# Four edits to a fused decoder layer: modulation sums split evenly between two engines, an early activation table, a divided half load, and two row blocks through other buffers

## The chip, the cores and the metric

The kernel runs on one core of one Trainium2 chip. The metric is the device time of one execution in microseconds (us), the median of several runs. Work is given to five engines that run side by side and wait for each other through semaphores: PE (matmuls), DVE and POOL (elementwise), ACT (activations and copies), and SP, which here issues the DMA transfers.

## The reference

One layer of a hybrid decoder on x (2048 x 1024, fp32) with a conditioning vector c:

```python
mod = jax.nn.silu(c) @ w_ada[layer] + b_ada[layer]
sh1, sc1, g1, sh2, sc2, g2 = jnp.split(mod[:, None, :], 6, axis=-1)
h = x * (1.0 + sc1) + sh1
proj = h @ w_in[layer] + b_in[layer]
...   # sliding-window attention and spatial gating on proj, joined to mixed
y = mixed @ w_out[layer]
x = layer_norm(ALPHA * x + g1 * y, ln1_g[layer], ln1_b[layer])
h = x * (1.0 + sc2) + sh2
gate, up = jnp.split(h @ w_gate_up[layer], 2, axis=-1)
y = (jax.nn.silu(gate) * up) @ w_down[layer]
x = layer_norm(ALPHA * x + g2 * y, ln2_g[layer], ln2_b[layer])
```

## The kernel before

All large products are done in three passes: each fp32 operand is split into a high part (a rounding copy, ACT, `split_hi`, L138) and a low part (the difference, DVE, `split_lo`, L141), and `mm3` (L144 to L146) issues high x high, one mixed product and the other mixed product, 128 x 128 by 128 x 512, into one PSUM bank.

The stages in order of time: a startup that makes the first two modulation vectors (`sh1`, `sc1`) in eight pieces k = 0 to 7 (`ada_ss`) and multiplies the first 512 rows of h with six column groups of the input weights, one k after the other (18 matmuls of 512 columns per k, 144 in all); a loop over the other rows with attention and gating; the out projection with the first LayerNorm, tile by tile (t = 0 to 15); the FFN's first product in two halves of the rows, each 11 steps `it` of seven products i = 0 to 6 (a Strassen-like scheme, products numbered n = 7 it + i); and the down product, a loop over seven combinations p with eight row blocks m each, 33 matmuls a block.

`ada_ss(k)` multiplies eight 128 x 256 weight pieces with c. For k = 0 all eight pieces are summed on PE, in 16 matmuls with one column; for the others DVE sums the first six (L225, L227), and PE does the last two and DVE's sum (L231, L233), six matmuls for two columns of output. L234 adds the bias; then `make_h` scales x (L193 on DVE) and splits it. Before the first product PE runs warm-up matmuls, 12 and then 8 (L323, L328), and a small product for the bias table (L325, copied by ACT at L326 and stored to `br_d`).

In the FFN `h_tiles(last_h2)` turns the last tiles of h over to the layout of the products: transposes on PE (L858) and eight copies on ACT (L861). It stands behind the product n = 0. `prep(n)` makes the weight combination of product n and its split two products ahead, `load_h(hf, i)` loads and splits the operand of product i in two pieces through a ring of two buffers (`hraw`: one in XF, and G1B). Between the halves `load_h(1, i)` follows each product of step it = 10. L1016 copies the accumulator Xg out of PSUM after a product; the first Silu is at L999.

In the down product `aprep(p, m)` loads row block m of operand p from `ac_d` through a ring of two buffers in F and splits it, one block ahead; `y_load` loads the residual rows into the tiles y. The FFN's last stores to `ac_d` and the weights' loads (L1106) are on the same queue.

The order of work on each engine is made by a scheduler from the program order, the buffers and its own priorities, except where `tc.keep_in_program_order` pins an instruction. Each engine executes its list in order; SP issues its transfers in order too, and a transfer is issued only when the eighth before it has landed.

Of the kernel before, what the change touches and what calls it, by code (L numbers as in the profile page):

```python
# [9 lines left out]
F32 = mybir.dt.float32  # L10
F32R = mybir.dt.float32r
U32 = mybir.dt.uint32
AF = mybir.ActivationFunctionType
ALU = mybir.AluOpType
# [10 lines left out]
WB = 255  # L25
# [32 lines left out]
def tile_layer(ctx, tc, xT, x, cT, wada_ss, wada4, bada_p, bada_g, win_g, win_a,  # L58
# [47 lines left out]
    def small(n, tag):  # L106
        return smalls.tile([P, n], F32, tag=tag, name=tag)
# [15 lines left out]
    expo = const(8)  # L123
# [11 lines left out]
    og = CS2[:, 22:30]  # L135

    def split_hi(hi, src, eng=None, **kw):
        (eng or A).activation(hi, src, AF.Copy, **kw)  # L138

    def split_lo(lo, src, hi, eng=None):  # L140
        (eng or V).tensor_tensor(lo, src, hi.bitcast(F32), op=ALU.subtract)  # L141

    def mm3(ps, lh, ll, rh, rl, start, stop, **kw):
        T.matmul(ps, lh, rh, start=start, stop=False, **kw)  # L144
# [60 lines left out]
    def load_wg(j, dst, pr, eng, r):  # L205
        r = load(r, win_g[j * 4 + pr])
        for i in range(2):
            hi, lo = dst[2 * pr + i]
            src = r[:, i * 512:(i + 1) * 512]
            split_hi(hi, src)  # L210
            split_lo(lo, src, hi, eng)

    def ada_ss(k):

        nd = 6 if k else 0
        ps = PS[7][:, 0:2]
        if k == 0:
            SY.dma_start(bap, bada_p)
            V.tensor_scalar(bap[:, 0:8], bap[:, 0:8], 1.0, None, op0=ALU.add)
            V.tensor_scalar(bap[:, 16:24], bap[:, 16:24], 1.0, None, op0=ALU.add)  # L220
        r = [load(ra0(), wada_ss[k, hf]) for hf in range(2)]
        piece = [r[rc // 4][:, rc % 4 * 256:rc % 4 * 256 + 256] for rc in range(8)]
        if nd:
            av = accs()
            V.tensor_scalar(av, piece[0], c_s[:, 0:1], None, op0=ALU.mult)  # L225
            for rc in range(1, nd):
                V.scalar_tensor_tensor(av, piece[rc], c_s[:, rc:rc + 1], av, op0=ALU.mult, op1=ALU.add)  # L227
        for j in range(2):
            js = slice(j * 128, (j + 1) * 128)
            for rc in range(nd, 8):  # L230
                T.matmul(ps[:, j:j + 1], piece[rc][:, js], c_s[:, rc:rc + 1], start=rc == nd, stop=rc == 7 and not nd)  # L231
            if nd:
                T.matmul(ps[:, j:j + 1], av[:, js], ones[:, 0:1], start=False, stop=True)  # L233
        V.tensor_tensor(mod.rearrange("p (j k) -> p k j", j=4)[:, k, 0:2], ps,  # L234
                        bap.rearrange("p (j k) -> p k j", j=4)[:, k, 0:2], op=ALU.add)

# [29 lines left out]
    def proj(ps, hT, t, k, w):  # L266
        hi, lo, _ = hT[k]
        mm3(ps, hi[:, t * 128:(t + 1) * 128], lo[:, t * 128:(t + 1) * 128], w[k][0], w[k][1],
            k == 0, k == KC - 1)
# [48 lines left out]
    SY.dma_start(relx, rel)  # L318
    SY.dma_start(ohx[:, 0:WB], onehot)
    warm = hbuf[7][2]  # L320
    V.memset(warm[:, 0:640].bitcast(F32), 0.0)
    for _ in range(12):
        T.matmul(PS[6], warm[:, 0:128], warm[:, 128:640], start=True, stop=True)  # L323
    prep0(0)
    T.matmul(PS[7][0:8, 256:256 + WB], relx, ohx[:, 0:WB], start=True, stop=True)  # L325
    A.activation(bstage, PS[7][0:8, 256:256 + WB], AF.Copy, scale=8.0)  # L326
    for _ in range(8):
        T.matmul(PS[6], wgv[0][0][:, 0:128], wgv[0][0], start=True, stop=True)  # L328
    for k in range(KC):
        if k + 1 < KC:  # L330
            prep0(k + 1)
        for t in range(6):
            proj(tiles0[t], hT, t % 4, k, wgv if t < 4 else wgu_)
    tc.keep_in_program_order(SY.dma_start(br_d, bstage))
    start_pool.__exit__(None, None, None)
    late_pool = tc.tile_pool(name="late", bufs=1)
# [493 lines left out]
    def load_h(hf, i, ring=hraw):  # L830
        hi, lo = HO[i]
        for h in range(2):
# [3 lines left out]
            split_hi(hi[:, hs], r)  # L836
            split_lo(lo[:, hs], r, hi[:, hs])

    def ln_stats(r):
        st, mv, rs = small(12, "st"), small(2, "mv"), small(1, "rstd")  # L840
        for h in range(2):
            V.bn_stats(st[:, h * 6:(h + 1) * 6], r[:, h * 512:(h + 1) * 512])
        V.bn_aggr(mv, st)
        V.tensor_scalar(rs, mv[:, 1:2], EPS, None, op0=ALU.add)  # L844
        G.tensor_tensor(rs, rs, expo[:, 0:1], op=ALU.pow)  # L845
        return mv, rs
# [64 lines left out]
    for t in range(NPRE, NT):  # L911
        if t + 1 < NT:
            stage_a(t + 1)
        r, xr, mx = loads[t]
        res = rr()
        st8 = wo_steps(t, xr, mx, res)
        for s_ in st8[0:8]:
            s_()
        if t + 1 < NT:
            mix_tr(loads[t + 1][0], loads[t + 1][2])  # L920
        for s_ in st8[8:16]:
            s_()
        h_tiles(ready)
        ready = []
        ln1(t, res)
        ready.append((t, res))
        if early:
            e = early.pop(0)
            re = rr()
            SY.dma_start(re, x1_d[e * P:(e + 1) * P, :])  # L930
            ln1(e, re)
            ready.append((e, re))
        if 3 < t < 12:
            rc = t - 4
            r = XF[:, 0:1024]
            SY.dma_start(r, wada4[3, rc])
            if rc == 0:
                V.tensor_scalar(G2B, r, c_s[:, 0:1], None, op0=ALU.mult)
            else:
                V.scalar_tensor_tensor(G2B, r, c_s[:, rc:rc + 1], G2B, op0=ALU.mult, op1=ALU.add)  # L940
            if rc == 7:
                SY.dma_start(r, bada_g[1:2, :].to_broadcast([P, D]))
                for h in range(2):
                    ps = trr()
                    T.matmul(ps, ones, G2B[:, h * 512:(h + 1) * 512], start=True, stop=True)
                    V.tensor_tensor(G2B[:, h * 512:(h + 1) * 512], ps, r[:, h * 512:(h + 1) * 512], op=ALU.add)
        if t in (10, 12):
            load_h(0, (t - 10) // 2, Ring([XF[:, 1024:2048]]))
    last_h2 = ready
# [102 lines left out]
    for n in range(NIT * 7):  # L1052
        it, i = divmod(n, 7)
        if n + 2 < NIT * 7:
            prep(n + 2)
        hi, lo = asl[n % 3]
        hh, hl = HO[i]
        for g in range(2):
            for j in range(4):
                ws = slice(g * 512 + j * 128, g * 512 + (j + 1) * 128)  # L1060
                hs = slice(j * 512, (j + 1) * 512)
                mm3(banks4[i][g], hi[:, ws], lo[:, ws], hh[:, hs], hl[:, hs],
                    first[i] and j == 0, j == 3, skip_group_check=not first[i])
        if n == 0:
            trr = Ring(PS[6:8])
            h_tiles(last_h2)
        post(n)
        if it == 10:
            load_h(1, i)
        fold_wd(i, it)  # L1070


# [45 lines left out]
        split_hi(hi, r)  # L1118
        split_lo(lo, r, hi)

    def aprep(p, m):
        r = arw()
        SY.dma_start(r, ac_d[p, m])
        hi, lo = at_()
        split_hi(hi, r)
        split_lo(lo, r, hi)
        return hi, lo

    def final(half, m, tail):
# [21 lines left out]
        tg = tile_of(half, m)  # L1151
        tc.keep_in_program_order(SY.dma_start(y[half][m], x1_d[tg * P:(tg + 1) * P, :]))

    nxt = aprep(seq[0], 0)
    for c in range(11):
        bsplit(0, c, bsum(0, c))
    y_load(1, 0)
# [2 lines left out]
    for n, p in enumerate(seq):  # L1160
        sums = []
        for m in range(8):
            ah, al = nxt
            if m < 7:
                nxt = aprep(p, m + 1)
            elif n < 6:
                nxt = aprep(seq[n + 1], 0)
            if n == 0:
# [98 lines left out]
```

## Time and profile before

| what | value |
|---|---|
| runs shown | 1971.59, 1974.17, 1976.45 us; median 1974.17 |
| profiled execution | 1973.5 us |
| its span, first to last instruction | 1971.5 us |
| PE busy | 1938.2 us (98%) |
| DVE, ACT busy | 1332.1 us (68%), 786.7 us (40%) |
| mean granted clock of PE | 0.99 |
| DMA | 354 MB on SP's queue, mean 180 GB/s |

The profile shows one execution. Rows of a timeline have the start and the duration in us, the engine, the source line, the operation, output and inputs, the shape and the count, and in brackets the idle time ahead with what ended it. SPq are SP's issues of transfers. Matmuls overlap, so their durations are longer than the distance of their starts. A one-column matmul of fp32 makes two records.

### The profile page before, as it was taken

The page shows a single profiled execution, that of the slowest core. Times are in us where ns is not written, and L with a number is a line of the kernel's source. Part 1 is how long each engine was busy: PE and PEld are TensorE (multiplying, and loading weights), DVE is VectorE, ACT ScalarE, POOL GpSimd, SP SyncE. Part 2 cuts the span into 40 slices and gives each one's busy share as a digit, 9 for nine tenths or more (in the row PEclk, how much of TensorE's full clock was granted, in tenths as well). Part 3 has the DMA queues.
Part 4 walks back from the last instruction along what each step waited for, and adds up shares of the span by engine and source line. Part 5 has one row for each costly group of instructions (what it writes and reads, how often), then busy time and mean ns, then how long its engine had stood idle before and what let it go on. Part 6 is the DMA issues. An engine that isn't in the chain of part 4 may idle for free.

```text
span 1971.5 us, 23966 instructions
## 1 busy us (share of the span) xinstructions
PE 1938.2 (98%) x8740; PEld 1585.2 (80%) x8740; DVE 1332.1 (68%) x2077; ACT 786.7 (40%) x1365; POOL 321.9 (16%) x285
## 2 busy tenths in 40 slices
PE   9999999999999999999999999999999899999998
PEld 7878878888878788888888788888888688888886
DVE  6675677996598776656666766566556665558856
ACT  3463346674355543333334433333334232224422
POOL 0545513564343100000000000000000000002303
PEclk8999999999999999999999999999999999999999
DMA  8763563533499764443445644434445985555623
GB/s 336 275 222 142 177 228 114 202 97 113 167 318 311 224 218 134 133 129 123 134 123 182 208 134 124 139 114 136 134 124 175 341 290 198 175 174 195 225 94 124
DMA packets 218399, 355.09 MB, mean 180 GB/s; under 512 B 14593, under 2 KB 124329, under 8 KB 218281
## 3 DMA queue, kind: packets, MB, share of 16 engines
q1 hardware_dynamic: 218280, 353.56, 54.0%
q8 instruction: 68, 1.11, 0.2%
q14 instruction: 51, 0.41, 0.1%
HBM read 242.88 MB, written 111.68 MB: 180 GB/s over the span
## 4 chain that ended last, share of the span: by engine, by line
PE 85%; DVE 6%; DMA 5%; ACT 2%; issue 2%; POOL 0%; SPq 0%; DVEq 0%; ACTq 0%; POOLq 0%
PE PS L144 26%; PE PS L146 26%; PE PS L145 26%; PE PS L626 2%; DVE R L141 2%; DMA RAW<-in_wada_dram 1%; ACT R L138 1%; PE PS L607 1%; PE PS L560 1%; PE PS L561 1%; DMA F<-ac_d 1%; DMA XF<-in_wada_dram 1%; DMA RAW<-in_xT_dram 1%; PE PS L858 1%; DMA G1B<-ht_d 0%
## 5 line engine op out<-in xcount | busy, mean ns | idle before, releaser
L145 PE MATMUL PS<-R 128*128 128x512 f32 (+1 forms) x1416 | 553.2, 391 | 0.3 <-DVE R L141 0.3
L144 PE MATMUL PS<-R 128*128 128x512 f32 (+1 forms) x1240 | 485.3, 392 | 9.3 <-ACT R L138 5.0
L146 PE MATMUL PS<-R 128*128 128x512 f32 (+1 forms) x1240 | 479.3, 389 | 3.3 <-DVE R L141 3.3
L145 PEld LDWEIGHTS PS<-R 128*128 128x128 f32 x1416 | 268.6, 190 | 56.7 <-DVE R L141 0.5
L141 DVE TENSOR_TENSOR R<-RAW,R 128x1024 fp32r<-128x1024 f32 (+1 forms) x212 | 217.6, 1041 | 126.6 <-ACT R L138 123.8
L138 ACT ACTIVATE R<-RAW 128x1024 fp32r<-128x1024 f32 (+1 forms) x232 | 202.8, 885 | 244.1 <-PE PS L145 191.6
L144 PEld LDWEIGHTS PS<-R 128*128 128x128 f32 x1240 | 235.5, 190 | 62.2 <-ACT R L138 7.3
L144 PE MATMUL PS<-R,R 128*128 128x512 f32 x688 | 275.1, 400 | 2.5 <-ACT R L138 1.3
L146 PEld LDWEIGHTS PS<-R 128*128 128x128 f32 x1240 | 233.8, 189 | 53.2 <-DVE R L141 5.0
L145 PE MATMUL PS<-R,R 128*128 128x512 f32 x688 | 273.6, 398 | 0.0
L146 PE MATMUL PS<-R,R 128*128 128x512 f32 x688 | 270.3, 398 | 0.3 <-DVE R L141 0.3
L845 POOL TENSOR_TENSOR rstd<-rstd,CS 128x1 f32<-128x1 f32 x32 | 35.3, 1105 | 1257.2 <-DVE rstd L844 1257.2
L144 PE MATMUL PS<-HA,R 128*128 128x512 f32 x528 | 208.7, 396 | 2.9 <-ACT R L138 2.9
L146 PE MATMUL PS<-HA,R 128*128 128x512 f32 x528 | 207.9, 395 | 0.4 <-DVE R L141 0.4
L138 ACT ACTIVATE R<-F 128x1408 fp32r<-128x1408 f32 (+2 forms) x86 | 105.4, 1229 | 226.5 <-PE PS L145 221.1
L144 PEld LDWEIGHTS PS<-R,R 128*128 128x128 f32 x688 | 130.4, 190 | 32.3 <-DMA R<-h_d 1.7
L146 PEld LDWEIGHTS PS<-R,R 128*128 128x128 f32 x688 | 130.0, 189 | 30.1 <-DVE R L141 0.7
L145 PEld LDWEIGHTS PS<-R,R 128*128 128x128 f32 x688 | 130.5, 190 | 28.4 <-issue 0.2
L141 DVE TENSOR_TENSOR R<-F,R 128x1408 fp32r<-128x1408 f32 (+2 forms) x86 | 132.0, 1537 | 22.9 <-ACT R L138 22.9
L145 PE MATMUL PS<-HA,R 128*128 128x512 f32 x352 | 138.9, 395 | 0.0
L1186 DVE TENSOR_TENSOR y<-y,PS 128x512 f32<-128x512 f32 x96 | 62.1, 682 | 104.5 <-PE PS L146 104.4
L969 DVE TENSOR_TENSOR F<-F,PS 128x512 f32<-128x512 f32 x132 | 89.8, 681 | 53.9 <-PE PS L146 52.6
(237 smaller groups left out, 2605.1 us busy)
## 6 DMA issues: line engine op xcount, KB each, us to landing
RAW<-in_wgu_dram SPq DMA_DIRECT2D x88, 512.0 KB, 3.9
ac_d<-fc SPq DMA_DIRECT2D x154, 256.0 KB, 2.6
F<-ac_d SPq DMA_DIRECT2D x56, 704.0 KB, 4.2
RAW<-wdg_d SPq DMA_DIRECT2D x100, 256.0 KB, 5.4
h_d<-R SPq DMA_DIRECT2D x32, 512.0 KB, 4.3
R<-h_d SPq DMA_DIRECT2D x32, 512.0 KB, 6.6
RAW<-in_wada_dram SPq DMA_DIRECT2D x24, 512.0 KB, 3.6
XF<-in_wd_dram SPq DMA_DIRECT2D x22, 512.0 KB, 4.5
```

Source lines behind the costliest of these rows:

```text
L138: (eng or A).activation(hi, src, AF.Copy, **kw)
L141: (eng or V).tensor_tensor(lo, src, hi.bitcast(F32), op=ALU.subtract)
L144: T.matmul(ps, lh, rh, start=start, stop=False, **kw)
L145: T.matmul(ps, lh, rl, start=False, stop=False, **kw)
L146: T.matmul(ps, ll, rh, start=False, stop=stop, **kw)
L560: T.matmul(b3[:, j, o:256], qh[:, qc], khh[kv][:, kc], start=True, stop=False)
L561: T.matmul(b3[:, j, o:256], qh[:, qc], klo[kv][:, kc], start=False, stop=True)
L607: T.transpose(tp[:, g * 128:(g + 1) * 128], p3[:, g, :], ident)
L626: T.matmul(psav, lh, rh, start=(kv == 0 and i == 0), stop=(kv == 1 and i == len(ms) - 1))
L845: G.tensor_tensor(rs, rs, expo[:, 0:1], op=ALU.pow)
L969: V.tensor_tensor(o, a, b, op=op)
L1186: V.tensor_tensor(ys, ys, ps, op=ALU.add if sign > 0 else ALU.subtract)
```

## The change

- `ada_ss`: for every k DVE sums four pieces and PE the other four and DVE's sum. k = 0 has ten one-column matmuls instead of 16, the others ten instead of six each.
- Warm-up: the memory is set to 1.0; the second group has five matmuls instead of eight and reads the same memory as the first. The bias table's product and copy follow the k loop. The splits of the first weight pair are pinned in order.
- A dummy Silu at tile 13 of the out projection calls for the table there.
- `h_tiles(last_h2)` follows n = 3 instead of n = 0.
- At it = 10 the loads of the second half are issued after each product (`load_hraw`), their splits (`split_h`) one product later.
- `aprep` takes the first row block in two halves of 704 columns through y[1][7] and y[1][6], the second through y[1][5] and y[1][4], tiles that nothing uses yet.

```diff
             src = r[:, i * 512:(i + 1) * 512]
-            split_hi(hi, src)
-            split_lo(lo, src, hi, eng)
+            a_ = split_hi(hi, src)
+            v_ = split_lo(lo, src, hi, eng)
+            if pr == 0:
+                tc.keep_in_program_order(v_)
+                if i == 1:
+                    tc.keep_in_program_order(a_)
...
-        nd = 6 if k else 0
+        nd = 4
...
-        if nd:
-            av = accs()
-            V.tensor_scalar(av, piece[0], c_s[:, 0:1], None, op0=ALU.mult)
-            for rc in range(1, nd):
-                V.scalar_tensor_tensor(av, piece[rc], c_s[:, rc:rc + 1], av, op0=ALU.mult, op1=ALU.add)
+        av = accs()
+        V.tensor_scalar(av, piece[0], c_s[:, 0:1], None, op0=ALU.mult)
+        for rc in range(1, nd):
+            V.scalar_tensor_tensor(av, piece[rc], c_s[:, rc:rc + 1], av, op0=ALU.mult, op1=ALU.add)
         for j in range(2):
             js = slice(j * 128, (j + 1) * 128)
             for rc in range(nd, 8):
-                T.matmul(ps[:, j:j + 1], piece[rc][:, js], c_s[:, rc:rc + 1], start=rc == nd, stop=rc == 7 and not nd)
-            if nd:
-                T.matmul(ps[:, j:j + 1], av[:, js], ones[:, 0:1], start=False, stop=True)
+                T.matmul(ps[:, j:j + 1], piece[rc][:, js], c_s[:, rc:rc + 1], start=rc == nd, stop=False)
+            T.matmul(ps[:, j:j + 1], av[:, js], ones[:, 0:1], start=False, stop=True)
...
-    V.memset(warm[:, 0:640].bitcast(F32), 0.0)
+    V.memset(warm[:, 0:640].bitcast(F32), 1.0)
     for _ in range(12):
         T.matmul(PS[6], warm[:, 0:128], warm[:, 128:640], start=True, stop=True)
     prep0(0)
-    T.matmul(PS[7][0:8, 256:256 + WB], relx, ohx[:, 0:WB], start=True, stop=True)
-    A.activation(bstage, PS[7][0:8, 256:256 + WB], AF.Copy, scale=8.0)
-    for _ in range(8):
-        T.matmul(PS[6], wgv[0][0][:, 0:128], wgv[0][0], start=True, stop=True)
+    for _ in range(5):
+        tc.keep_in_program_order(T.matmul(PS[6], warm[:, 0:128], warm[:, 128:640], start=True, stop=True))
     for k in range(KC):
         if k + 1 < KC:
             prep0(k + 1)
         for t in range(6):
             proj(tiles0[t], hT, t % 4, k, wgv if t < 4 else wgu_)
+    T.matmul(PS[7][0:8, 256:256 + WB], relx, ohx[:, 0:WB], start=True, stop=True)
+    A.activation(bstage, PS[7][0:8, 256:256 + WB], AF.Copy, scale=8.0)
     tc.keep_in_program_order(SY.dma_start(br_d, bstage))
...
+    def load_hraw(hf, i):
+        rs = []
+        for h in range(2):
+            r = hraw()
+            SY.dma_start(r.rearrange("p (j c) -> p j c", j=2), ht_d[hf, i][:, 2 * h:2 * h + 2, :])
+            rs.append(r)
+        return rs
+
+    def split_h(i, rs):
+        hi, lo = HO[i]
+        for h, r in enumerate(rs):
             hs = slice(h * 1024, (h + 1) * 1024)
             split_hi(hi[:, hs], r)
             split_lo(lo[:, hs], r, hi[:, hs])
...
+        if t == 13:
+            tc.keep_in_program_order(A.activation(small(1, "sw"), expo[:, 0:1], AF.Silu))
...
-        if n == 0:
+        if n == 3:
             trr = Ring(PS[6:8])
             h_tiles(last_h2)
         post(n)
+        if (it, i) == (11, 0):
+            split_h(6, h_next)
         if it == 10:
-            load_h(1, i)
+            if i > 0:
+                split_h(i - 1, h_next)
+            h_next = load_hraw(1, i)
...
-    def aprep(p, m):
-        r = arw()
-        SY.dma_start(r, ac_d[p, m])
+    def aprep(p, m, via=None):
         hi, lo = at_()
-        split_hi(hi, r)
-        split_lo(lo, r, hi)
+        if via is None:
+            pieces = [(arw(), 0, 1408)]
+        else:
+            pieces = [(y[1][j][:, 0:704], h * 704, (h + 1) * 704) for h, j in enumerate(via)]
+        for r, c0, c1 in pieces:
+            SY.dma_start(r, ac_d[p, m][:, c0:c1])
+        for r, c0, c1 in pieces:
+            split_hi(hi[:, c0:c1], r)
+            split_lo(lo[:, c0:c1], r, hi[:, c0:c1])
...
-    nxt = aprep(seq[0], 0)
+    nxt = aprep(seq[0], 0, (7, 6))
...
-                nxt = aprep(p, m + 1)
+                nxt = aprep(p, m + 1, (5, 4) if (n, m) == (0, 0) else None)
```

What the scheduler makes of it, at three places. On DVE, at the start, before: R is a split weight or h, st raw data, L234 the sum of the modulation, L193 the scaling of x.

```order
L220 TENSOR_SCALAR CS<-CS 128x8
L141 TENSOR_TENSOR R<-st,R 128x512 x2
L234 TENSOR_TENSOR CS<-PS_84,CS 128x2
L193 TENSOR_SCALAR st<-st,CS 128x512
L141 TENSOR_TENSOR R<-st,R 128x512 x2
```

The same place now, with L228 and L230 the sum of four pieces and L236 the former L234:

```order
L224 TENSOR_SCALAR CS<-CS 128x8
L228 TENSOR_SCALAR F<-RAW,CS 128x256
L230 SCALAR_TENSOR_TENSOR F<-RAW,CS,F 128x256 x3
L236 TENSOR_TENSOR CS<-PS_84,CS 128x2
L193 TENSOR_SCALAR st<-st,CS 128x512
L141 TENSOR_TENSOR R<-st,R 128x512 x5
```

The modulation's sum stood behind two splits and now stands ahead of all.

On ACT, at the start of the FFN, before. L861 are the copies of `h_tiles`, L999 is Silu, R<-RAW are splits of weights (the second is that of product n = 2, which PE takes up next), R<-XF and R<-G1B splits of h:

```order
L138 ACTIVATE R_108<-G1B 128x1024
L861 ACTIVATE fc_4301<-PS_83,CS 128x128 x4
L861 ACTIVATE fc_4301<-PS_84,CS 128x128 x4
L999 ACT_TABLE_LOAD
L999 ACTIVATE F<-F 128x512
L138 ACTIVATE R<-XF 128x1024
L138 ACTIVATE R<-RAW 128x1024 x2
L138 ACTIVATE R<-G1B 128x1024
```

Now, with L1018 the Silu and L878 the copies of `h_tiles`; the split of product n = 2 is the R<-RAW behind these:

```order
L138 ACTIVATE R_108<-G1B 128x1024
L1018 ACTIVATE F<-F 128x512
L138 ACTIVATE R<-RAW 128x1024
L138 ACTIVATE R<-XF 128x1024
L878 ACTIVATE fc_4310<-PS_83,CS 128x128 x4
L878 ACTIVATE fc_4310<-PS_84,CS 128x128 x4
L138 ACTIVATE R<-RAW 128x1024
L138 ACTIVATE R<-G1B 128x1024
```

The table load left the place, and the Silu and two splits passed the eight copies; the split of n = 2 did not.

On SP, where the FFN ends, before: F<-ac_d is the first row block of the down product, y_0 the first residual rows.

```order
L1123 DMA F<-ac_d 128x1408
L993 DMA ac_d<-fc_4301 128x4x128
L1042 DMA wdg_d<-XF 128x1024
L1159 DMA G2B<-in_ln2b_dram 128x1024
L1106 DMA RAW<-wdg_d 128x512 x2
L1106 DMA F<-wdg_d 128x512
L1106 DMA RAW<-wdg_d 128x512
L1152 DMA y_0_10655<-x_d 128x1024
L1106 DMA RAW<-wdg_d 128x512
L993 DMA ac_d<-fc_4301 128x4x128 x2
L1123 DMA F<-ac_d 128x1408
```

Now: y_7 and y_6 take the halves of the first row block, y_5 and y_4 those of the second, and F<-ac_d at the head is the third.

```order
L1151 DMA F<-ac_d 128x1408
L1012 DMA ac_d<-fc_4310 128x4x128
L1061 DMA wdg_d<-XF 128x1024
L1187 DMA G2B<-in_ln2b_dram 128x1024
L1129 DMA RAW<-wdg_d 128x512 x2
L1129 DMA F<-wdg_d 128x512
L1129 DMA RAW<-wdg_d 128x512
L1151 DMA y_7_10673<-ac_d 128x704
L1151 DMA y_6_10672<-ac_d 128x704
L1012 DMA ac_d<-fc_4310 128x4x128 x2
L1180 DMA y_0_10666<-x_d 128x1024
L1151 DMA y_5_10671<-ac_d 128x704
```

The load at the head now serves a later block, and the first block's loads stand eight places behind it.

Around the half change, from the split of the second piece of i = 3 to that of i = 5, the rows of ACT, SP and PE stand in the same order as before. On SP the store of the bias table, `br_d`, stood among the last loads of the startup; now it stands behind all of these and ahead of the stores of h. The transposes of `h_tiles` on PE stood inside product n = 1 and now follow it.

More of the change, by code (lines that the diff above doesn't have):

```diff
@@ L137, in split_hi @@
     def split_hi(hi, src, eng=None, **kw):
-        (eng or A).activation(hi, src, AF.Copy, **kw)
+        return (eng or A).activation(hi, src, AF.Copy, **kw)
     def split_lo(lo, src, hi, eng=None):
-        (eng or V).tensor_tensor(lo, src, hi.bitcast(F32), op=ALU.subtract)
+        return (eng or V).tensor_tensor(lo, src, hi.bitcast(F32), op=ALU.subtract)
     def mm3(ps, lh, ll, rh, rl, start, stop, **kw):
@@ L837, in load_h @@
             split_lo(lo[:, hs], r, hi[:, hs])
+    def load_hraw(hf, i):
[8 more added lines that the diff above has]
+        for h, r in enumerate(rs):
+            hs = slice(h * 1024, (h + 1) * 1024)
+            split_hi(hi[:, hs], r)
+            split_lo(lo[:, hs], r, hi[:, hs])
     def ln_stats(r):
```

## The prediction

> **What bounds the kernel now.** I read the page's totals, then the granted clock by stage, then PE's waits, and only then the timelines around the four places that the change touches.
>
> ```profile
> span 1971.5 us, 23966 instructions
> PE 1938.2 (98%) x8740; PEld 1585.2 (80%) x8740; DVE 1332.1 (68%) x2077; ACT 786.7 (40%) x1365; POOL 321.9 (16%) x285
> ```
>
> PE is the bound. A gain is a PE wait removed, or a stretch of low clock removed, and nothing else. The stages (columns: busy time and count of PE, PEld, DVE, ACT, POOL, then the clock):
>
> ```profile
> 0.00:68.00 68.00, 64.25 (x284) 52.73 (x285) 44.02 (x100) 24.87 (x40) 3.76 (x8) 0.85 0.87 330
> 680.00:695.00 15.00, 11.66 (x44) 8.82 (x43) 10.91 (x11) 11.85 (x18) 0.00 (x0) 0.89 0.66 201
> 1087.00:1097.00 10.00, 6.85 (x23) 5.16 (x23) 9.71 (x10) 5.82 (x9) 0.00 (x0) 0.83 0.70 227
> 1528.00:1567.00 39.00, 31.94 (x120) 23.83 (x119) 25.98 (x35) 11.61 (x13) 0.00 (x0) 0.91 0.94 338
> ```
>
> The clock is either 1.00 or 0.50, so a mean of 0.85 over 68 us is 20.4 us at half clock; the other rows give 3.3, 3.4 and 7.0 us, that is one, one and two stretches of 3.4 us.
>
> ```profile
> 685.08 0.40 PE L146 MATMUL PS<-R,R 128*128 128x512 f32 x1
> 688.38 0.50 PE L144 MATMUL PS<-HA,R 128*128 128x512 f32 x1 [2.90 <-ACT R L138]
> 690.02 0.80 PE L146 MATMUL PS<-HA,R 128*128 128x512 f32 x1 [0.44 <-DVE R L141]
> 692.32 0.63 PE L145 MATMUL PS<-R 128*128 128x512 f32 x1
> 692.74 0.53 PE L146 MATMUL PS<-HA,R 128*128 128x512 f32 x1
> 693.11 0.39 PE L144 MATMUL PS<-HA,R 128*128 128x512 f32 x1
> 693.34 0.39 PE L145 MATMUL PS<-R 128*128 128x512 f32 x1
> ```
>
> Starts are 0.23 us apart at full clock (693.11 to 693.34) and 0.42 cold (692.32 to 692.74): 0.20 us lost per cold 512-column matmul, eight of them or 1.6 us per stretch of 3.4.
>
> **Startup.** Before, the 16 one-column matmuls of the first modulation were over early, but their sum waited on DVE:
>
> ```profile
> 7.03 3.79 PE L231 MATMUL PS<-CS,RAW 128*128 128x1 f32 x32
> 16.24 0.79 PE L144 MATMUL PS<-R 128*128 128x512 f32 x1
> 11.57 1.29 DVE L141 TENSOR_TENSOR R<-st,R 128x512 fp32r<-128x512 f32 x2 [7.32 <-ACT R L138]
> 12.78 0.15 DVE L234 TENSOR_TENSOR CS<-PS,CS 128x2 f32<-128x2 f32 x1
> 10.90 2.44 ACT L138 ACTIVATE R<-st 128x512 fp32r<-128x512 f32 x4 [8.23 <-DMA st<-in_win_g_dram]
> 13.55 0.63 ACT L138 ACTIVATE R<-st 128x512 fp32r<-128x512 f32 x1 [0.20 <-DVE st L193]
> ```
>
> One such matmul costs 3.79/16 = 0.24 us (two records). The second half of its weights was there by 7.03 + 4 x 0.24 = 8.0 us, since the fifth matmul reads it. With ten instead of 16, PE is done by about 10.3, and DVE, where the sum now stands ahead of the weight splits, adds it at once. The split of h then waits only on ACT, behind two halves of the weight that arrives at 10.90: 10.90 + 3 x 0.6 = 12.6 us. The first product starts there instead of at 16.24: 3.6 us earlier. The five warm-up matmuls (5 x 0.42 = 2.1 us) fit between 10.3 and 12.6, and the bias-table matmul, moved to the end of the stage, costs about 0.6 us there.
>
> Against that, k = 1 to 7 each have ten one-column matmuls in PE's stream instead of six: 28 x 0.24 = 6.7 us more. DVE loses two of its sums per k, but PE pays. The budget of the stage: 12.6 + 144 products x 0.23 (33.1) + 70 x 0.24 (16.8) + 0.6 = 63.1 us, plus waits, plus the cold clock. Before, the stage ended at 67.5. One-column matmuls count little for the clock, as these rows tell:
>
> ```profile
> 20.60:37.70 17.10, 16.18 (x94) 14.03 (x93) 13.24 (x32) 4.80 (x9) 0.00 (x0) 1.00 1.03 409
> 37.70:41.10 3.40, 3.40 (x9) 2.62 (x9) 3.40 (x7) 2.37 (x5) 0.00 (x0) 0.50 1.03 410
> 48.77 0.50 PE L231 MATMUL PS<-CS,G1B 128*128 128x1 f32 x4
> 52.20 0.77 PE L144 MATMUL PS<-R,R 128*128 128x512 f32 x1
> 51.30:58.10 6.80, 6.80 (x20) 5.54 (x20) 4.79 (x10) 4.41 (x7) 0.00 (x0) 0.50 0.76 212
> ```
>
> PE ran nothing but such matmuls from 48.77 to 52.20, and 6.8 cold us follow. Afterwards k = 1 and 2 stand back to back (20 of them, 4.8 us: I count one cold stretch, 1.6 us), the others stand alone (2.4 us each, shorter than what cooled it before: half a stretch in all, 0.8), and the first products run cold as they do now, about five of them (1.0 us). 63.1 + 3.4 + 0.5 of waits = 67.0: **a gain of 0.5 to 1.5; I take 1.0.** Ends: no cold stretch and no wait past k = 0, +3.5; three stretches more than I count, -3.5.
>
> What else moves is the store of the bias table. On SP it now stands ahead of ten stores of h and the loads of the next rows' x, and waits for PE's moved matmul, at about 62 us:
>
> ```profile
> 57.05 10.56 SPq L203 DMA_DIRECT2D h_d<-R  x10
> 67.67 1.19 SPq L184 DMA_DIRECT2D RAW<-in_xT_dram  x1
> ```
>
> So these come some 5 us later: the load at 73, in use by about 82. PE's new order puts 96 products (22 us) between the end of the stage and the first that reads it: 89. This cover of 7 us hides it; were it gone, it would cost up to 5.
>
> **FFN start.** The idle 3.07 us (688.38 less 685.08 less 0.23) is ACT's queue:
>
> ```profile
> 667.52 2.90 ACT L861 ACTIVATE fc<-PS,CS 128x128 f32<-128x128 f32 x8 [6.83 <-PE PS L858]
> 680.66 2.88 ACT L861 ACTIVATE fc<-PS,CS 128x128 f32<-128x128 f32 x8
> 683.56 1.28 ACT L999 ACT_TABLE_LOAD   x1
> 686.34 1.99 ACT L138 ACTIVATE R<-RAW 128x1024 fp32r<-128x1024 f32 x2
> ```
>
> PE waits for the second of the two at 686.34, which ends at 688.33. In the new order the table load is gone from here and the Silu and two splits come ahead of the eight copies, but the copies still stand ahead of the split that PE waits for. So it moves up by the load alone, 1.28 us, and no more, although h_tiles was moved three steps back in the code: done at 687.05, PE idle 1.8 us. PE's second wait, 0.44 for the low half, shrinks too, since no other split stands ahead of this one on DVE any more: I take 0.3 of it. The load now falls into idle ACT time such as the 6.83 us ahead of 667.52; without that cover it would cost its 1.28 again. A hole of 1.8 us, where 3.1 cooled the clock, probably no longer does: 1.6. **Gain 3.1 (1.28 + 0.3 + 1.6, rounded down); ends 1.3 (still cold) and 4.5 (the whole wait).**
>
> The Trainium skill, "TensorE: Matmul & The Clock Gate", Part 1 and the summary table, says that the clock halves after a free-running window of about 3.4 us spent idle, and that gaps above some 3 us are to be avoided. The trace is stricter: 2.90 and 3.15 us of wait sufficed, shorter than a window. By the page alone the 1.8 us hole is warm, and each burst of 2.4 us in the startup too: 0.8 us less than my sum.
>
> **Half change.**
>
> ```profile
> 1091.26 0.50 PE L144 MATMUL PS<-R 128*128 128x512 f32 x1 [3.15 <-ACT F L1016]
> 1089.67 1.06 ACT L138 ACTIVATE R<-G1B 128x1024 fp32r<-128x1024 f32 x1 [2.01 <-DMA G1B<-ht_d]
> 1085.03 0.32 SPq L834 DMA_DIRECT2D G1B<-ht_d  x1
> ```
>
> PE waits for ACT's copy L1016, which stands behind a split whose data, issued at 1085.03, was there at 1089.67. The change takes the split out of the load and runs it a step later. But the loads still share two buffers, each is issued only when the split of the buffer's last content is done, and in the built order load, split and copy stand here as before; only what lies behind them moves. What hid nothing before hides nothing now. **Gain 0; ends -1.6 and +4.7** (3.15 + 1.6, if the split did leave the copy's way).
>
> **Down start.**
>
> ```profile
> PE PS L144 <- ACT R L138: 3.8, 4, 1.3
> PE PS L146 <- DVE R L141: 3.3, 3, 1.4
> 1521.94 0.50 SPq L1123 DMA_DIRECT2D F<-ac_d  x1
> 1528.91 1.38 ACT L138 ACTIVATE R<-F 128x1408 fp32r<-128x1408 f32 x1 [2.14 <-DMA F<-ac_d]
> 1528.62 0.39 PE L146 MATMUL PS<-R 128*128 128x512 f32 x1
> 1528.89 0.32 SPq L1152 DMA_DIRECT2D y<-x_d  x1
> y<-x_d SPq DMA_DIRECT2D x3, 512.0 KB, 7.5
> ```
>
> Seven waits of 7.1 us, each 0.16 more in starts (8.2), and two cold stretches (3.2): 11.4 us lost from 1528 to 1567. The new code's first row block comes in halves through y tiles. But in the built order those loads do not stand where the first load stood: that place (issued 1521.94) now fetches the third row block, and the halves stand where y[1][0]'s load was issued at 1528.89. It was issued when the transfer eight places ahead of it landed, and the new load waits for the same one. DMA is as good as full there (0.94, 338 GB/s in the stage's row), and 512 KB took 7.5 us to landing, to 1536.4. A half is 352 KB, 160 KB or 0.5 us less: 1535.9, and 1.0 later the second. ACT takes 0.7 for a half (1.38 for the whole): PE starts at 1536.6, a hole of 7.8 us after its last FFN matmul (1528.62 + 0.23), where the wait is 1.3 now. Then 0.4 for the low half and a full cold start of 3.4 to 6.8 us (1.6 to 3.2, I take 2.4): 10.6 lost. The second block's halves follow by 1541 and the third is long there, so the other five waits and the second cold stretch go. **Gain 0.8; ends -3 (halves 2 us later, longest cold start) and +5 (halves 4 us earlier).** After that a block's split waits for PE to free its buffer, one block ahead, which leaves a block of 33 x 0.23 = 7.6 us for 1.4 on ACT and as much on DVE. y[1][0] and its neighbours load two places later; they are read at the end of a block, 9 us on.
>
> **The sum.** 1.0 + 3.1 + 0 + 0.8 = 4.9 us less than the profiled execution's 1973.5 us, which lies 0.7 under the median of the runs shown: **1968.6**. What a measurement here can tell from no change is about 0.3%, 5.9 us: the bound is at 1968.2, so the likeliest case lies on that edge.
>
> **Rivals.** (1) The startup and the FFN hole stay cold: 0 to -1 and 1.5, with the down start even: **1972**. For it: seven longer bursts; against: the pair of k = 6 and 7 that cooled the clock at 51.3 stands apart in the new order. Chance 0.22. (2) A part works as it is meant to: the half change's wait goes, or the halves land by 1532, with the startup at its good end: 4.9 + 4 to 6, **1963**. For it: PE's waits there are only on loads; against: the built order. Chance 0.24. (3) Slower: the startup's one-column bursts, one per 18 products, leave no window full enough, and all 144 products run cold, where now 20.4 us are; about 100 products x 0.20 = 20 us more, **1989**. It decides from some 60 more cold products on (12 us and the 4 gained elsewhere). For it: 3.4 us of such matmuls cost 6.8 cold us at 51.3; against: 20.60 to 37.70 kept its 1.00 although the bursts of k = 1 to 4 lie in it. Chance 0.06. My own case: 0.48, spread 1966 to 1971.
>
> By the Trainium skill's window (the page named above) rival 3 would not come, since a burst of 2.4 us never fills 3.4.
>
> **How the numbers follow.** My case splits about evenly at 1968.2, rival 2 is faster, rival 1 the same, rival 3 slower: faster 0.25 + 0.24 = 0.49, same 0.23 + 0.22 = 0.45, slower 0.06. The range 1962 to 1973 holds my case and most of rivals 1 and 2.
>
> **What would show it.** First product at 12.6 us, and the stage's last product near 67; table load ahead of 660; FFN hole of 1.8 us with clock 1.00 after; the half change's hole of 3.1 us unchanged; a single hole of 7 to 8 us at the down start, then 33-matmul blocks without waits. Wrong if the half change's hole is gone, if the first down load is issued by 1522, or if the startup has over three cold stretches.

## The result, and the profile after

The changed kernel takes 1951.38 us (median of five runs, 1950.08 to 1955.9) against 1973.47 for the kernel before: a ratio of 0.9893 (95% interval 0.9880 to 0.9906), 21 us less by the ratio. The prediction was 1968.6, with 1962 to 1973 as its range; the chance of "faster" was given as 0.49. So the direction was the likelier one and the size was missed by 17 us. The profiled execution of after took 1953.6 us.

The page's totals of after, and PE's longest waits (us in total, times, longest):

```profile
span 1951.5 us, 24038 instructions
PE 1920.9 (98%) x8781; PEld 1589.7 (81%) x8781; DVE 1330.8 (68%) x2069; ACT 784.1 (40%) x1368; POOL 320.7 (16%) x285
```

```profile
PE PS L144 <- ACT R L138: 12.8, 5, 7.9
PE PS L144 <- ACT F L1035: 2.4, 1, 2.4
PE PS L144 <- DVE F L703: 2.4, 1, 2.4
PE PS L325 <- DVE R L323: 1.8, 1, 1.8
```

PE's busy time fell by 17.3 us (1938.2 to 1920.9) though it has 41 instructions more. A wait removed is idle time and cannot do that, and a cold stretch less is worth 1.6 us by the prediction's rows. So I set the start of the N-th matmul of L144 to L146 of after against that of before (7752 in each; 96 of them have 256 columns, the others 512): N = 144, the startup's end, 5.5 us later; N = 600, 0.3 later; N = 2100, 3.8 earlier; N = 2400, behind the FFN's start, 6.2 earlier; N = 5850, the FFN's end, 18.3 earlier; N = 6150, behind the down start, 20.1 earlier, and constant from there. Twelve of the 20 us come in small even steps all through the FFN, where the change edits nothing but the half change. The windows by stage show it, first before, then after (columns as in the prediction's stage table; the count behind PE is that of its instructions):

```profile
700.00:1060.00 360.00, 360.00 (x1568) 294.10 (x1567) 228.50 (x264) 124.04 (x161) 0.00 (x0) 1.00 0.45 137
```

```profile
700.00:1060.00 360.00, 360.00 (x1590) 298.17 (x1589) 234.06 (x270) 125.70 (x164) 0.00 (x0) 1.00 0.45 140
```

Both have PE busy without a gap at full clock, but a matmul comes every 360/1568 = 0.2296 us before and every 0.2264 after. The groups of instructions by form in the same 360 us (behind the first bar: busy us, then mean ns of one) name the slow ones. Before:

```profile
L144 PE MATMUL PS<-R 128*128 128x512 f32 x234 | 91.1, 389 | 0.0
L144 PE MATMUL PS<-HA,R 128*128 128x512 f32 x216 | 85.0, 394 | 0.0
L144 PE MATMUL PS<-R,R 128*128 128x512 f32 x72 | 28.4, 394 | 0.0
```

After:

```profile
L144 PE MATMUL PS<-R 128*128 128x512 f32 x225 | 87.5, 389 | 0.0
L144 PE MATMUL PS<-HA,R 128*128 128x512 f32 x233 | 90.5, 389 | 0.0
L144 PE MATMUL PS<-R,R 128*128 128x512 f32 x72 | 28.0, 389 | 0.0
```

The same instruction on the same shape took 394 ns where one operand lies in HA or in R1 (the second R of "R,R"), and 389 where both lie in R; all three are tiles of split operands. After, all take 389. In distances of starts, which is what PE pays, it is 232 to 233 ns against 227. The change adds one tile that its description does not dwell on: the dummy Silu's output `small(1, "sw")`. A new tag in the pool of small tiles takes 4 x 32 = 128 bytes of each partition, and in the built programs every tile allocated behind that pool on the same side of the memory moves by these 128 bytes: R1 from 142720 to 142848, XF (and R2) from 159104 to 159232, HA from 169344 to 169472. Modulo 256 they go from 128 to 0. R, at 59392, lay at 0 before and after. That was the theory for the experiments; the rival was that the edits themselves act.

### The profile page after: what moved, and what is told of

The parts are those of the page before. It is cut to its first block, busy times and chain, and to the rows that moved or that the text cites. A ratio compares the mean times of both kernels' runs of the same rounds, so it can differ in the third digit from the quotient of the medians.

```text
span 1951.5 us, 24038 instructions
## 1 busy us (share of the span) xinstructions
PE 1920.9 (98%) x8781; PEld 1589.7 (81%) x8781; DVE 1330.8 (68%) x2069; ACT 784.1 (40%) x1368; POOL 320.7 (16%) x285
## 4 chain that ended last, share of the span: by engine, by line
PE 84%; DVE 7%; DMA 3%; issue 2%; ACT 2%; POOL 1%; SPq 0%; DVEq 0%; POOLq 0%; ACTq 0%
PE PS L144 26%; PE PS L145 26%; PE PS L146 26%; DVE R L141 2%; PE PS L628 1%; DMA G1B<-ht_d 1%; ACT R L138 1%; PE PS L234 1%; PE PS L563 0%; PE PS L562 0%; PE PS L609 0%; PE PS L875 0%; DMA RAW<-in_x_dram 0%; DMA y<-ac_d 0%; DVE G2B L397 0%
## 5 line engine op out<-in xcount | busy, mean ns | idle before, releaser
L144 PE MATMUL PS<-R 128*128 128x512 f32 (+1 forms) x1240 | 484.5, 392 | 12.2 <-ACT R L138 9.8
L146 PE MATMUL PS<-R 128*128 128x512 f32 (+1 forms) x1240 | 480.3, 389 | 0.1
L144 PEld LDWEIGHTS PS<-R 128*128 128x128 f32 x1240 | 235.7, 190 | 62.3 <-ACT R L138 11.0
L144 PE MATMUL PS<-R,R 128*128 128x512 f32 x688 | 272.0, 396 | 4.6 <-DVE F L703 2.4
L146 PEld LDWEIGHTS PS<-R 128*128 128x128 f32 x1240 | 234.9, 190 | 49.1 <-DVE R L141 1.2
L146 PE MATMUL PS<-R,R 128*128 128x512 f32 x688 | 269.0, 394 | 0.0
L144 PE MATMUL PS<-HA,R 128*128 128x512 f32 x528 | 206.1, 391 | 1.7 <-ACT R L138 1.7
L146 PE MATMUL PS<-HA,R 128*128 128x512 f32 x528 | 205.8, 391 | 0.1
L144 PEld LDWEIGHTS PS<-R,R 128*128 128x128 f32 x688 | 129.7, 189 | 31.7 <-DVE F L703 2.6
L146 PEld LDWEIGHTS PS<-R,R 128*128 128x128 f32 x688 | 129.7, 188 | 26.7 <-issue 0.2
L145 PE MATMUL PS<-HA,R 128*128 128x512 f32 x352 | 136.9, 389 | 0.0
L1214 DVE TENSOR_TENSOR y<-y,PS 128x512 f32<-128x512 f32 x96 | 62.3, 683 | 103.3 <-PE PS L146 103.3
```

The costliest lines, as they stand in the source:

```text
L145: T.matmul(ps, lh, rl, start=False, stop=False, **kw)
L146: T.matmul(ps, ll, rh, start=False, stop=stop, **kw)
L1214: V.tensor_tensor(ys, ys, ps, op=ALU.add if sign > 0 else ALU.subtract)
```

## Experiments

Times are medians. The ratio, with its 95% interval, is to the kernel before in the same session; 0.001 is 2 us.

### The shift alone, and the change without it

The shift alone (`b_pad128`) is the kernel before with one line:

```diff
+    small(8, "pad")
     cpos = [0]
```

> The kernel before with one unused small tile more, so that the tiles allocated behind the small ones (R1, st, R2, XF, HA, y) lie 128 bytes further on, at multiples of 512 bytes; every engine has the same instructions in the same order. Address theory: 512-column matmuls that read these tiles issue every 0.227 us instead of 0.233, 12 us less in the FFN (22 steps x 88 matmuls x 0.006) and up to 9 more ahead of it: 1953 to 1961 us, and 360/1590 = 0.2264 us per matmul in the FFN. Rival, that the edits to the order made after faster: no change, 1973 us within 3, and 0.2296 us per matmul in the FFN.

The change without the shift (`a_nosw`):

```diff
-            tc.keep_in_program_order(A.activation(small(1, "sw"), expo[:, 0:1], AF.Silu))
+            tc.keep_in_program_order(A.activation(small(1, "nmr"), expo[:, 0:1], AF.Silu))
```

> The kernel after, with the dummy Silu written to a small tile of a kind that exists already, so that nothing is shifted; all engines have the same instructions in the same order as after. Address theory: the 12 to 21 us come back, 1963 to 1972 us, and what is left of the gain is the four edits alone (my sum said 4.9). Rival: 1951 us, as after.

The shift alone: 1956.59 us, 0.9935 (0.9918 to 0.9951). The change without it: 1965.83, 0.9977 (0.9963 to 0.9991), that is 4.5 us faster, 1.8 to 7.3. The FFN's window of the one, then of the other:

```profile
700.00:1060.00 360.00, 360.00 (x1590) 298.08 (x1589) 232.55 (x268) 125.85 (x164) 0.00 (x0) 1.00 0.46 141
```

```profile
700.00:1060.00 360.00, 360.00 (x1566) 293.83 (x1566) 230.13 (x266) 123.91 (x161) 0.00 (x0) 1.00 0.45 137
```

An unused tile gives after's pitch (the distance of starts), and the four edits without it have before's. From N = 2400 to 5850 the shift alone gains 12.0 us and `a_nosw` 0.6. This settles it: 12.8 of the 21 us (9.7 to 16.2) are addresses; the edits as meant are worth 4.5 where I had summed 4.9. The remaining 4 us between 12.8 + 4.5 and 21 lie within these intervals. That 4.5 meets 4.9 is in part luck (see the sum, below).

### Which addresses are good

`a_offsets` cuts HA into five tiles (high and low part of products i = 0 and 1, high part of i = 2) with gaps between them:

```diff
-    HA = ffn.tile([P, 10240], F32R, name="HA")
+    HA = []
+    for i, pad in enumerate((0, 8, 8, 16, 32)):
+        if pad:
+            ffn.tile([P, pad], F32, name=f"hp{i}")
+        HA.append(ffn.tile([P, 2048], F32R, name=f"HA{i}"))
...
```

> The kernel after with the FFN's tile HA cut into five tiles with gaps, so that they begin at 0, 32, 64, 128 and 256 bytes past a multiple of 512; same instructions in the same order. If only a multiple of 512 is fast: 48 of 168 matmuls a step are 0.006 us slower, 22 x 48 x 0.006 = 6.3 us, 1957 to 1958 us. If a multiple of 256 does: 32 of them, 4.2 us. If a multiple of 64 does: 8 of them, 1.1 us. If the address plays no part: 1951 us and one pitch of 0.227 for all five.

1955.47 us, 0.9922 (0.9900 to 0.9945). 1500 matmuls of the FFN take 342.5 us, against 340.0 after and 344.9 before: 6.2 us for all 3696. By the sum alone that is the "512" case. But the mean distances of starts between 760 and 1040 us, by product, say otherwise (`here` is `a_offsets`; the other operand of each matmul lies in R, at 0):

| product i | offsets, high and low part | ns here | ns before | ns after |
|---|---|---|---|---|
| 0 | 0 and 32 | 231.7 | 232.9 | 226.7 |
| 1 | 64 and 128 | 232.4 | 233.4 | 226.7 |
| 2 | 256 and 0 | 227.9 | 229.4 | 226.7 |
| 4 to 6 | 0 and 0 | 226.7 | 227.3 | 226.7 |

32, 64 and 128 are bad, and 256 is clean: of the 24 matmuls of i = 2 only the first six, right behind i = 1, are slower, and the other 18 issue every 226.7 ns. One bad operand in three matmuls slows its neighbours as well: i = 0 counts in full, which my counts for the cases had left out. That is no general rule, since in before i = 2 has two bad ones in three and takes only 229.4. `a_all256` confirms 256, below. One rival stays untested: in every 512-column matmul of the three-pass products one operand lies in R, at a multiple of 256 in every kernel here, so these runs do not tell an address that is bad by itself from two operands that differ modulo 256.

### The startup

`a_oldstart` gives after the startup of before back. `a_hybrid` changes one line of after:

```diff
-        nd = 4
+        nd = 6 if k else 4
```

`b_start` is the shift with the new startup alone.

> The kernel after with the startup of before (six sums on DVE for k = 1 to 7 and none for k = 0, the old warm-up, the bias table's product ahead). The trace of after ends its startup at 73.0 us against 67.6 before. Theory that this loss reaches the end: 1946 us, 5.5 less than after, last startup product near 67.5. Rival, that the loop behind takes it back (the two traces are level again by the 600th product): 1951 us.

> The kernel after, but for k = 1 to 7 DVE sums six pieces again and PE has six one-column matmuls instead of ten; k = 0 stays at four and four, with the new order at the start. Three executions of the new startup end it at 73.0, 68.6 and 67.6 us, three of the old one at 67.6, 65.1 and 62.3. Theory that the 28 extra one-column matmuls cost (28 x 0.24 = 6.7 us and cold clock): first product still at 12.6, end of the startup 60 to 65, in all 1944 to 1947 us. Rival, that the early start itself leaves the clock cold: end at 67 to 73 as in after, 1951 us.

> The kernel before with the 128-byte shift and the new startup alone (four sums on each engine for every k, the new warm-up, the bias table's product behind the loop, the pinned splits); to be set against the shift alone, 1956.6 us. By the traces so far the startup of 144 products ends 3 to 7 us later than the old one, and the stretch up to the 600th product then takes 2 us less, since two waits on the next rows' h are gone: 1957 to 1961 us, the last startup product at 67 to 73. Rival, my prediction's term: 1 us less than without it, 1955.6, and an end near 65.

Measured: `a_oldstart` 1948.36, 0.9901 (0.9877 to 0.9925), against after's 0.9893; `a_hybrid` 1947.57, 0.9881 (0.9869 to 0.9894); `b_start` 1956.22, 0.9920 (0.9903 to 0.9937), against 0.9935 for the shift alone. No pair can be told apart by time: what the startup edit does lies within some 5 us of nothing. The traces are finer. In four executions of the new startup (after, `a_nosw`, `a_offsets`, `b_start`) it ends at 73.0, 68.6, 67.6 and 67.8 us; in six of the old one at 62.3 to 67.6, mean 64.8; and in three of the hybrid's (it comes back in two kernels below) at 66.7, 63.1 and 66.6. The 28 extra one-column matmuls cost about 4 us there, which is the direction of the hybrid's theory, although only one of its three ends falls into the 60 to 65 that it expected. The earlier first product brings nothing: the hybrid starts it at 12.7 to 13.9 us, the old startup at 14.9 to 16.8, and they end alike. By N = 600 about 2 us are back. The gating products (256 columns) wait at 128 to 138 us in the shift alone, with 1.05 and 1.2 us between starts, and these waits are shorter or gone in the new order. `b_start` fits neither of its two cases in full: its time is nearer to the rival's 1955.6, its end is that of the expected case.

`a_break` asks whether it is the length of the bursts of one-column matmuls that cools the clock. It adds, in the loop over `rc`:

```diff
+                if k and rc in (5, 7):
+                    tc.keep_in_program_order(T.matmul(PS[6], wgv[0][0][:, 0:128], wgv[0][0], start=True, stop=True))
```

> The kernel after with four more 512-column matmuls (their product isn't used) in the one-column bursts of each k = 1 to 7, two in each column's, so that no more than 0.7 us of one-column matmuls stand together. Theory that bursts of 2.2 us and more cool the clock now and then: after the first products no cold stretch is left; 3 to 4 stretches of 3.4 us less (5 to 6 us), for 28 x 0.23 = 6.4 us of added matmuls: startup ends at 67 to 70, in all 1950 to 1953 us. Rival, that the share of time in which PE works at full width counts and not the length of a burst: the cold stretches stay, and it is slower by the 6.4 us and more, 1956 to 1960.

1957.05 us, 0.9937 (0.9916 to 0.9958): 6 to 9 us slower than after (by the medians and by the ratios), as the rival had it. Windows of after (a burst of 2.15 us, what follows it, and a later stretch with one such burst in it) and of `a_break` (k = 1 and 2 back to back, what follows, k = 3 to 7, and the end):

```profile
39.50:41.80 2.30, 2.30 (x22) 2.26 (x21) 1.81 (x4) 2.04 (x4) 0.00 (x0) 1.00 0.17 53
42.20:45.60 3.40, 3.40 (x9) 2.64 (x8) 3.37 (x7) 0.64 (x1) 0.00 (x0) 0.50 0.82 296
50.00:60.20 10.20, 10.20 (x56) 8.78 (x55) 5.58 (x12) 5.13 (x8) 0.00 (x0) 1.00 0.00 0
```

```profile
18.60:22.50 3.90, 3.65 (x30) 3.40 (x28) 1.27 (x5) 1.15 (x2) 0.00 (x0) 1.00 1.03 420
22.50:32.80 10.30, 10.30 (x34) 8.82 (x34) 9.68 (x22) 3.53 (x7) 0.00 (x0) 0.50 1.03 418
34.20:66.70 32.50, 32.50 (x195) 28.66 (x194) 12.27 (x27) 7.46 (x12) 0.00 (x0) 1.00 0.26 102
66.90:70.30 3.40, 3.40 (x9) 2.65 (x8) 2.00 (x4) 2.22 (x5) 0.00 (x0) 0.51 0.93 296
```

With no more than about 0.7 us of one-column matmuls together the clock still halves, in the middle of the double unit and once behind a single one. In after one burst of 2.15 us cools it, the next two do not, and the one after these does. So the length of a burst does not decide.

The traces show more than this experiment asked for. In all fourteen the granted clock changes only at marks that lie 3.41 us apart. In after, bursts that begin at 39.5 and 60.3 us lie whole between two marks (38.75 and 42.16, 59.23 and 62.64), and half clock follows; those that begin at 47.5 and 53.9 are cut by a mark (48.99, 55.81), and the clock stays at 1.00. Count each 512-column matmul at full clock as 0.227 us, and one that a mark cuts in part. Then of the stretches between marks at full clock in the fourteen startups, 44 were followed by half clock, all filled to 0.383 or less with such matmuls, and 146 were not, all filled to 0.388 or more. The two stretches of `a_break` ahead of its half clock were filled to 0.22 and 0.38. This is a count over traces at hand; no run was made to test the limit.

### The other parts alone, on the shift

`b_silu` is before with the dummy Silu's two lines, `b_half` has the divided load, `b_down` the two row blocks through y, each with the shift and nothing else.

> The kernel before with the dummy Silu alone, whose small tile brings the 128-byte shift with it; to be set against the shift alone, 1956.6 us. My step: the wait at the FFN's start shrinks by the table load's 1.28 us, to a hole of about 1.8, with 1 to 3 us gained in all, 1954 to 1956 us, although h_tiles stays where it was. Rival, that moving h_tiles is what helps: hole of 3.1 us and a cold stretch as before, 1956.6.

> The kernel before with the 128-byte shift and the load of the second half's operands divided into load and split, nothing else of the change. My step: the copy that PE waits for at the half change still stands behind a split whose data come late: hole of 2.8 to 4.3 us and a cold stretch as without the edit, no gain, 1956 us within 3. Rival, that the division frees the copy: hole below 1 us, 3 to 5 us less, 1952.

> The kernel before with the 128-byte shift and the first two row blocks of the down product through the y tiles, nothing else of the change. My step: a single hole of 7 to 8 us in place of seven waits, 0.8 less than the shift alone (ends -3 and +5), 1953 to 1957 us. Rival, that the gain of 2 to 4 us which the traces of the changed kernels show at this place needs the other edits: 1956.6.

Measured: 1954.44, 0.9925 (0.9911 to 0.9940); 1955.22, 0.9926 (0.9902 to 0.9949); 1953.38, 0.9914 (0.9900 to 0.9927). Against 0.9935 these are gains of 2, 2 and 4 us, with 4 to 6 of uncertainty, so no time alone tells them from nothing. The places in the traces are clear. PE's timeline in `b_silu` and in `b_half`, and PE's longest wait in `b_down`:

```profile
675.77 0.50 PE L144 MATMUL PS<-HA,R 128*128 128x512 f32 x1 [1.54 <-ACT R L138]
677.41 0.50 PE L146 MATMUL PS<-HA,R 128*128 128x512 f32 x1 [0.43 <-DVE R L141]
684.05 0.50 PE L144 MATMUL PS<-R 128*128 128x512 f32 x1 [1.80 <-ACT F L1015]
```

```profile
1077.17 0.79 PE L145 MATMUL PS<-R 128*128 128x512 f32 x1 [3.23 <-ACT F L1032]
```

```profile
PE PS L145 <- ACT R L139: 14.0, 4, 7.9
```

The early table load takes 1.23 us from the FFN's first wait (2.77 in the shift alone, 1.54 here) with h_tiles where it was: the step held. But the next wait, 1.80, now cools the clock, so the cold stretch stayed (the stretch between marks with the wait of 1.54 was filled to 0.43, that with 1.80 to 0.39), and the distance from N = 2100 to 2400 is 78.4 us, no less than in the shift alone (77.1) or before (78.5). With h_tiles moved as well it is 75.4 to 76.8 in the eight executions that have both edits; in the five that have the shift without both it is 76.3 to 78.4. So the move of h_tiles, to which I gave nothing, may have a part in the gain; it wasn't tried alone. The half change waits 3.23 as before (3.15). The down start has its single hole of 7.9.

### The addresses of all tiles, and a better version

`a_all256` is the hybrid with pads so that every large tile begins at an odd multiple of 256 (R, R1, HA and BX at 256 modulo 512):

```diff
+    statics.tile([P, 32], F32, name="pad0")
+    rpad = ctx.enter_context(tc.tile_pool(name="rpad", bufs=1, side="right"))
+    rpad.tile([P, 56], F32, name="pad1")
     F = Arena(statics.tile([P, NF0], F32, name="F"))
...
+    statics.tile([P, 32], F32, name="pad2")
     R = Arena(statics.tile([P, NA], F32R, name="R"))
```

> The kernel of the hybrid startup, with every tile, those of the right side too, at a multiple of 256 bytes; same instructions in the same order. Address theory: the weights of the down product that lie in BX (411 of 1848 matmuls, 233.5 instead of 227 ns) and the attention's operands (pitch 228.5 instead of 226.7 between 260 and 680 us) issue at 227 too: 2.8 + 2 = 4 to 5 us less than the hybrid, some 1941 us. Rival, that 512 is the multiple that counts: R1, HA and y then lie badly again, and it is 12 us slower than the hybrid.

1943.42, 0.9864 (0.9850 to 0.9879), against the hybrid's 1947.57 and 0.9881: by time alone 3 to 4 us, at the edge of the noise. Groups by form from 1560 to 1900 us, the hybrid, then this:

```profile
L144 PE MATMUL PS<-R 128*128 128x512 f32 x388 | 151.2, 390 | 0.0
L144 PE MATMUL PS<-fx,R 128*128 128x512 f32 x108 | 42.8, 396 | 0.0
```

```profile
L148 PE MATMUL PS<-R 128*128 128x512 f32 x388 | 151.0, 389 | 0.0
L148 PE MATMUL PS<-fx,R 128*128 128x512 f32 x112 | 43.6, 389 | 0.0
```

BX (fx), which lay at 224 modulo 256 in both kernels, was slow in both; now it is not, and the down product from N = 6150 to 7300 takes 2.5 us less. 256 suffices: 1500 matmuls of the FFN take 340.0 here with HA at an odd multiple, and the rival's 12 us more did not come. The part on the attention was wrong: its pitch stayed at 228.5.

`c_swap` takes that kernel and gives the down product's first block back to F, and the second and third to the y tiles:

```diff
-    nxt = aprep(seq[0], 0, (7, 6))
+    nxt = aprep(seq[0], 0)
...
-                nxt = aprep(p, m + 1, (5, 4) if (n, m) == (0, 0) else None)
+                nxt = aprep(p, m + 1, (7, 6) if (n, m) == (0, 0) else (5, 4) if (n, m) == (0, 1) else None)
```

> The kernel with the hybrid startup and all tiles at multiples of 256 bytes, but the first row block of the down product comes again through F, at the head of SP's queue, and the second and third come in halves through the y tiles. In the changed kernels PE has a hole of 8.3 us at the down start and then 9 to 11 cold matmuls. My step, that the place of the first load in the queue sets this hole: hole below 2 us, one stretch of cold clock less, and perhaps a wait of up to 2 us for the second block: 5 to 8 us less than the 1943.4 of the same kernel without this, 1936 to 1939. Rival, that DMA is full there and a load gained at one place is lost at the next: holes as large at the second block, 1943.

1937.10 us, 0.9837 (0.9814 to 0.9859): 32 us faster than before, and it beats after too. Against `a_all256` it is 5 to 6 us, at the edge of the noise by time alone. SP's queue, then PE, in after:

```profile
1503.79 0.50 SPq L1151 DMA_DIRECT2D F<-ac_d  x1
1510.25 1.15 SPq L1151 DMA_DIRECT2D y<-ac_d  x2
```

```profile
1518.60 0.80 PE L144 MATMUL PS<-R 128*128 128x512 f32 x1 [7.90 <-ACT R L138]
```

and in `c_swap`:

```profile
1496.80 2.11 SPq L1155 DMA_DIRECT2D F<-ac_d  x1
1505.28 0.32 SPq L1155 DMA_DIRECT2D y<-ac_d  x1
```

```profile
1505.89 0.50 PE L148 MATMUL PS<-R 128*128 128x512 f32 x1 [1.99 <-ACT R L142]
1507.56 0.80 PE L150 MATMUL PS<-R 128*128 128x512 f32 x1 [0.93 <-DVE R L145]
```

The early place in the queue now fetches what PE needs first. The hole shrinks from 7.9 to 1.99 + 0.93, the blocks behind it run without waits, and N = 5850 to 6150 takes 74.3 us instead of 79.1 in `a_all256`, 78.5 in after and 80.3 in before. The cold stretch did not go; it moved behind the shorter hole (13 cold matmuls).

## Why the prediction was wrong, point by point

- **The step that failed** is none of the four terms but the premise ahead of them: "A gain is a PE wait removed, or a stretch of low clock removed, and nothing else." The largest gain is neither. The distance of starts at full clock, which I took as 0.23 us for every product from a pair of rows with HA, itself became shorter: 0.2296 to 0.2264 us on average in the FFN. Of the 21 us, 12.8 are that. I costed the dummy Silu as an ACT instruction and never asked where its output tile lies and what moves behind it. The trace of before showed what there was to gain: forms of the same instruction at 389 and 394 ns.
- **Startup, +1.0 predicted.** First product at 12.6: it came at 12.69. End at 67.0: 73.0, 68.6, 67.6 and 67.8. The term that was mis-sized is the cold clock: I counted 17 cold products, and 42, 28, 26 and 25 of the 144 start at half clock. At 0.2 us each that is 5 us more in after, whose end is 6.0 late, and about 2 in the others, 0.6 to 1.6 late. Of the first products 9 to 13 ran cold, where I counted five (before itself has ten). Behind them after has five cold stretches of 3.4 us and the others two each, where I counted one and a half and named more than three as a sign of being wrong. And the gain was worked out from one execution of before, whose end at 67.6 is the latest of the six old ones; against their mean the new startup loses 3 to 8 us. The window 10.4 to 73 us of after:

```profile
10.40:73.00 62.60, 61.08 (x291) 51.56 (x290) 36.17 (x77) 22.05 (x37) 0.36 (x1) 0.81 0.66 257
```

  Rival 3, that all 144 run cold, did not come; its mechanism, windows not full enough, is what the extra cold stretches show. By the Trainium skill ("TensorE: Matmul & The Clock Gate", Part 1) a window must be idle for the clock to fall, and no burst here could do it; the trace differs, with 3.4 us at 0.50 right behind a burst in which PE was never idle. The same page calls the window free-running, so that the count of cold matmuls changes from run to run; with 25 to 42 for the same startup in four kernels, the trace agrees.
- **The bias table's later store** was to be hidden, with a risk of 5 us. It was; the loop behind even gained about 2.
- **FFN start, +3.1.** Worked out as in the prediction, the hole is 1.9 us in after (682.53 less 680.41 less 0.23), where 1.8 was predicted; in `a_nosw` it is 0.9. The low half's wait, 0.44 before, is about 0.2 in after (683.33 to 683.79, less a distance of 0.23) but 0.56 in `a_nosw`. The clock halved all the same at 683.9 in after; in `a_nosw`, where the hole was smaller, it did not. From N = 2100 to 2400 `a_nosw` gains 2.6.
- **Half change, 0.** Right: a wait of 2.42 on the same copy in after, 3.23 in `b_half`, and a cold stretch in each.
- **Down start, +0.8.** The hole of 7.8 was 7.9, the other waits went, the cold start was 11 matmuls, 2.2 us. From N = 5850 to 6150 `a_nosw` gains 0.9, and `b_down` 2.8 over the shift alone.
- **The sum.** 4.9 was predicted for the edits and 4.5 (1.8 to 7.3) measured without the shift. That they meet is in part luck: in the trace of `a_nosw` the startup ends 1.1 us later than in before, where 1.0 earlier was counted, and by N = 2100 it is 6.4 us ahead, which no term holds, while the median of its ten runs shows 4.5 in all. The prediction's range had no room for a cause that is in no term.

## What to carry to other kernels

When a change adds, drops or resizes any tile, list the addresses of all tiles allocated behind it; a difference that grows evenly over a whole stage and has no place of its own is a sign of it. In a profile, compare the mean ns of one instruction between forms of equal shape: if only the tile differs and the time does too, look at that tile's address. And before a load is given another buffer, look at where it lands in the transfer queue; the block that is needed first should have the earliest place.

## What was not expected of the hardware

- In the FFN and the down product a 512-column fp32 matmul issued every 226.7 ns with both operands at multiples of 256 bytes in the partition, and every 231 to 234 on average with one at 32, 64, 128 or 224 past such a multiple, apart from the mixed product i = 2 of before (229.4). In the FFN (HA, R1) that operand is the streamed one; in the loop of the first product it is the stationary h, 395 ns a form before and 389 shifted:

```profile
L144 PE MATMUL PS<-R,R 128*128 128x512 f32 x60 | 23.7, 395 | 0.0
```

```profile
L145 PE MATMUL PS<-R,R 128*128 128x512 f32 x59 | 23.0, 389 | 0.0
```

  The first row is from before, the second from the shift alone. What in the chip makes it so stays open, as does the attention's 228.5.
- The clock halved after waits of 1.7 to 2 us and after stretches without any idle time, for 3.4 us or two or three times that, and only at marks 3.41 us apart. What separates the two cases in the startups is how much of the 3.41 us ahead of a mark 512-column matmuls filled: 0.383 at most against 0.388 at least.
